# Down projection of a streaming encoder's feed-forward layer: from eight block products to seven, with the weight sums made in device memory

## The chip, the cores and the metric

The kernel runs on one core of a Trainium2 chip. The metric is the device time of one execution in microseconds. Before the change the median of three runs is 1411.47 us (1410.40 to 1413.36).

## The reference, cut to what matters

One inference step of a one-layer encoder: a mixer (three kinds of gated recurrences), then a convolutional feed-forward layer, each between two RMS norms. There are 1024 prompt rows and 32 sample rows, D_MODEL is 1024 and D_FF 2816. All arrays are fp32. The change is in the last step, the product with `w_down`, and what follows it:

```
def conv_ffn(xn, buf, w_up, conv_w, conv_b, w_down):
    up = xn @ w_up
    up, buf = causal_dwconv(up, buf, conv_w, conv_b)
    gate, val = jnp.split(up, 2, axis=-1)
    return (jax.nn.gelu(gate, approximate=True) * val) @ w_down, buf
...
        h, ffn_buf = conv_ffn(rms_norm(x, g_ffn_pre[l]), states[6][l], ffn_w_up[l], ffn_conv_w[l],
                              ffn_conv_b[l], ffn_w_down[l])
        x = x + rms_norm(h, g_ffn_post[l])
```

So the down projection is (1056 x 2816) times (2816 x 1024), then a norm over each row of 1024 and the residual.

## The kernel before

The kernel is written with a planner: the program names tiles in pools, and the planner places them, sets the order of each engine's instructions from dependencies, priorities (the order of writing) and its own timeline, and adds the waits. `tc.issue_after` is the hand-written way to keep an instruction behind another one; it is used in a few places, none of them in the down projection. SP issues nearly all DMAs, in one queue.

Every large product is made in fp32r from split operands. `split` writes a high half with ACT (a cast) and a low half with DVE (source minus high half), and `mm3` multiplies high by high, high by low and low by high into one PSUM bank. A block of 128 x 128 by 128 x N thus costs three products of TensorE.

The stages in order:

- The input projection and the mixer fill the first 690 us. The input projection's weights come from device memory, are split, and the low halves are stored there (`lt_d`, `lf_d`) and read again for the later groups of rows.
- The up projection runs from about 690 to 1146 us. `up_all` goes over 22 blocks `f` of 128 hidden columns (a gate and a value block each) and over two halves `s` of the rows. Each block already uses seven products (`PROD`) instead of eight on quarter blocks; the sums of its weights are made by DVE in SBUF (`up_operands`). `up_finish` does the convolution, the gelu and the product, with four small POOL copies ahead of each ACT step, and stores block `f` of the hidden rows to `h_d[f]` (128 hidden x 1060 columns of rows, the prompt in two halves with a gap, the sample in the middle).
- The down projection `down_all` takes three groups of rows (`DGROUPS`): (0, 1, 8), (2, 3, 4) and (5, 6, 7), where 8 is the sample. For each group it goes over the 22 hidden blocks again: `load_h` loads that group's rows of `h_d[f]` and all of `w_dn[f]` (512 KB), and splits them. In the first group the weights are the stationary operand and 288 rows are streamed, so the result is transposed back afterwards (`turned`); in the other two groups the rows are stationary and 512 weight columns are streamed. `finish` does the norm and the residual (`residual` loads rows of `x2_d`). In the last group the last four blocks are kept back (`n_end`) and applied bank by bank, so that the banks close one after the other.

The tag `raw` holds two raw weight tiles, `op` seven split ones. `ahead` prepares the first two blocks of the down projection while the up projection ends.

Of the kernel before, what the change touches and what calls it, by code (L numbers as in the profile page):

```python
# [18 lines left out]
SEQ = 1024  # L19
DEC = 32  # L20
# [14 lines left out]

DGROUPS = [(0, 1, 8), (2, 3, 4), (5, 6, 7)]

# [53 lines left out]
def body(ctx: ExitStack, tc: tile.TileContext, a: dict):  # L91
# [45 lines left out]
    h_d = dr.tile([NF, 128, NCOL], F32, name="h_d")  # L137

# [1203 lines left out]
    def up_all(pw_, W0, X, uus, py, ahead, begun):  # L1342

        raw, W = {}, {0: W0}
        late = None
        for f in range(NF):
# [3 lines left out]
            for s in range(2):  # L1350
# [25 lines left out]
    def load_h(ph, g, f, spans, w, deep=None):  # L1376
        r = ph.tile([128, 384], F32, tag="hr", name=f"hr{g}_{f}", bufs=2)
        for (c0, c1, o) in spans:
            sp.dma_start(r[:, o:o + c1 - c0], h_d[f, :, c0:c1])
        hh = ph.tile([128, 384], F32R, tag="hh", name=f"hh{g}_{f}", bufs=4)  # L1380
        hl = ph.tile([128, 384], F32R, tag="hl", name=f"hl{g}_{f}", bufs=4)
        split(hh[:, :w], hl[:, :w], r[:, :w], dve)
        wr = praw[0].tile([128, 1024], F32, tag="raw", name=f"wd{g}_{f}r", bufs=2)
        sp.dma_start(wr, a["w_dn"][f])
        return hh, hl, [weight_halves(f"wd{g}_{f}{hf}", wr[:, 512 * hf:512 * hf + 512], deep) for hf in range(2)]

    def spans_of(us):
        spans, off, w = [], {}, 0
        for u in us:
            n = 128 if u < 8 else DEC  # L1390
            off[u] = w
            if spans and spans[-1][1] == fcol(u):
                spans[-1][1] += n
            else:
                spans.append([fcol(u), fcol(u) + n, w])
            w += n
        return spans, off, w

    def down_all(ph, p6, gp, begun):
        xres = {}  # L1400

        def residual(u):
            n = 128 if u < 8 else DEC
            x = p6.tile([128, 1024], F32, tag="xres", name=f"fr{u}", bufs=4)
            sp.dma_start(x[:n], x2_d[128 * u:128 * u + n, :])
            xres[u] = x

        def finish(u, n, src):

            x = xres.pop(u)  # L1410
            ss = p6.tile([128, 4], F32, tag="fss", name=f"gss{u}", bufs=4)
            jk = p6.tile([128, 1024], BF16, tag="fjk", name=f"gjk{u}", bufs=2)
            ys = []
            for hf in range(2):
                c = slice(512 * hf, 512 * hf + 512)
                act.activation(jk[:n, c], src[hf], AF.Square, accum_out=ss[:n, 2 + hf:3 + hf])  # L1416
                y = p6.tile([128, 512], F32, tag="yt", name=f"yt{u}{hf}", bufs=4)
                dve.tensor_tensor(y[:n], src[hf], gp[:n, c], op=ALU.mult)
                ys.append(y)
            pool.tensor_tensor(ss[:n, 0:1], ss[:n, 2:3], ss[:n, 3:4], op=ALU.add)  # L1420
            rstd_of(ss[:n, 1:2], ss[:n, 0:1], n, 1, 1024)
            for hf in range(2):
                c = slice(512 * hf, 512 * hf + 512)
                dve.scalar_tensor_tensor(x[:n, c], ys[hf][:n], ss[:n, 1:2], x[:n, c], op0=ALU.mult, op1=ALU.add)
                sp.dma_start(a["yp"][128 * u:128 * u + n, c] if u < 8 else a["ys"][:, c], x[:n, c])

        def banks_of(g, m):

            where = [(psf, "xw", 4)] * 4 + [(psb, "big", 3)] * 3 + [(psf, "sx", 1)]
            return [p.tile([128, 512], F32, tag=t, name=f"pd{g}_{i}", bufs=b) for i, (p, t, b) in enumerate(where[:m])]  # L1430


        us = DGROUPS[0]
        spans, off, w = spans_of(us)
        banks = banks_of(0, 8)
        for f in range(NF):
            hh, hl, wd = begun.pop(f, None) or load_h(ph, 0, f, spans, w)
            if f == NF - 4:
                for u in us:
                    residual(u)  # L1440
            for d in range(8):
                c = slice(128 * (d % 4), 128 * (d % 4) + 128)
                mm3(banks[d][:, :w], [t[:, c] for t in wd[d // 4]], (hh[:, :w], hl[:, :w]), f == 0, f == NF - 1)
        acc = p6.tile([128, 8, 288], F32, name="accd")
        for d in range(8):
            (act.copy if d % 2 else dve.tensor_copy)(acc[:, d, :], banks[d][:, :w])

        def turned(u):
            n = 128 if u < 8 else DEC
            src = []  # L1450
            for hf in range(2):
                p, t, b = ((psb, "big", 3), (psf, "sx", 1))[hf]
                ps = p.tile([128, 512], F32, tag=t, name=f"pt{u}{hf}", bufs=b)
                for d in range(4):
                    pe.transpose(ps[:n, 128 * d:128 * d + 128], acc[:, 4 * hf + d, off[u]:off[u] + n], ident)
                src.append(ps[:n])
            finish(u, n, src)

        todo = [lambda u=u: turned(u) for u in us]
        for g, us2 in enumerate(DGROUPS[1:], 1):  # L1460
# [10 lines left out]
            for f in range(NF):  # L1471
                ops = load_h(ph, g, f, spans, w, p6 if f >= NF - n_end // 2 else None)
                if f == NF - 4:
                    for u in us2:
                        residual(u)
# [286 lines left out]
```

## Time and profile before

| | |
|---|---|
| median of three runs | 1411.47 us |
| span of the profiled execution (the page gives no other time of it) | 1409.0 us |
| TensorE busy | 1366.7 us, 97% |
| DVE busy | 1009.7 us, 72% |
| ACT busy | 711.2 us, 50% |
| POOL busy | 299.0 us, 21% |
| moved by DMA | 255.10 MB, mean 181 GB/s |
| first and last product of the down projection | 1146.27 us, 1402.27 us |

The page divides the span into 40 slices of 35 us. In its rows a digit is the busy share of a slice in tenths. A group's line ends with the idle time of its engine just before the group's instructions and with what ended most of it. SPq is SP's queue of DMA issues.

### The profile page before, as it was taken

How to read it: one execution, taken by the hardware profiler on the slowest of the kernel's cores; microseconds unless marked ns; L12 is line 12 of the kernel's file. 1: busy time of each engine (PE TensorE's matmuls, PEld its weight loads, DVE VectorE, ACT ScalarE, POOL GpSimd, SP SyncE). 2: the span in 40 equal slices, each digit the busy share in tenths (PEclk: the TensorE clock that was granted, in tenths of full speed). 3: DMA queues.
4: the chain of work that ended last, by engine and by line, in shares of the span. 5: the costliest groups of instructions: out<-in, count | busy, mean ns of one | idle time of the engine just before them, and what ended most of it. 6: DMA issues, size and time to landing. Idle time of an engine off the chain costs nothing.

```text
span 1409.0 us, 30015 instructions
## 1 busy us (share of the span) xinstructions
PE 1366.7 (97%) x11804; PEld 1252.3 (89%) x11804; DVE 1009.7 (72%) x1818; ACT 711.2 (50%) x1399; POOL 299.0 (21%) x497
## 2 busy tenths in 40 slices
PE   6999999999999999999899999999999999999998
PEld 5999889898888987777799999999999999988886
DVE  4786478758687669777798788788878865654644
ACT  4555447445474545334755555455545445543432
POOL 5532311235211245212131111111111110000100
PEclk9999999999999989999999999999999999999999
DMA  9599879785899744445312222222122267764752
GB/s 346 191 335 351 273 236 304 229 273 189 271 274 347 243 160 142 137 135 144 123 55 96 99 82 76 77 79 88 63 91 77 70 208 224 245 220 166 247 177 101
DMA packets 129444, 255.10 MB, mean 181 GB/s; under 512 B 27639, under 2 KB 74263, under 8 KB 129303
## 3 DMA queue, kind: packets, MB, share of 16 engines
q1 hardware_dynamic: 122839, 244.54, 52.2%
q10 hardware_dynamic: 4800, 4.33, 0.9%
q0 software_dynamic: 1664, 4.33, 0.8%
q8 instruction: 92, 1.51, 0.4%
q14 instruction: 49, 0.40, 0.1%
HBM read 192.26 MB, written 60.89 MB: 180 GB/s over the span
## 4 chain that ended last, share of the span: by engine, by line
PE 79%; DVE 9%; DMA 4%; ACT 4%; issue 2%; POOL 1%; SPq 1%; DVEq 0%; POOLq 0%; ACTq 0%
PE pd L102 6%; PE pd L101 6%; PE pd L100 6%; PE pux L100 4%; PE pux L102 4%; PE pux L101 4%; PE pv L100 4%; PE pv L102 4%; PE pv L101 4%; PE puw L101 3%; PE puw L100 3%; PE puw L102 3%; PE mi L718 2%; PE zp L100 2%; PE zp L102 2%; PE zp L101 2%
## 5 line engine op out<-in xcount | busy, mean ns | idle before, releaser
L1336 DVE SCALAR_TENSOR_TENSOR y<-uu,fconv_sb,y 128x1060 f32<-128x1060 f32 x88 | 116.3, 1321 | 28.3 <-ACT y L1334 27.6
L102 PE MATMUL pd<-wd,hl 128*128 128x512 f32 x264 | 105.0, 399 | 0.0
L101 PE MATMUL pd<-wd,hh 128*128 128x512 f32 x264 | 104.1, 394 | 0.0
L100 PE MATMUL pd<-wd,hh 128*128 128x512 f32 x264 | 103.4, 393 | 0.0
L1330 POOL COPY uu<-uu 128x2 f32<-128x2 f32 x44 | 36.7, 834 | 214.4 <-DVE uu L1278 214.2
L1273 ACT COPY c<-pux 128x274 f32<-128x274 f32 (+1 forms) x132 | 49.3, 376 | 40.8 <-PE pux L102 39.8
L100 PE MATMUL pv<-wt_0h,xh 128*128 128x256 f32 (+2 forms) x195 | 57.8, 297 | 6.8 <-ACT xh L319 4.8
L1334 ACT ACTIVATE y<-uu,fconv_sb 128x1060 f32<-128x1060 f32 x44 | 56.1, 1275 | 16.0 <-POOL uu L1331 15.4
L100 PE MATMUL zp<-woh,ch 128*128 128x512 f32 (+1 forms) x144 | 59.2, 412 | 1.9 <-DVE z L1154 1.2
L101 PEld LDWEIGHTS pd<-wd,hh 128*128 128x128 f32 x264 | 49.6, 188 | 12.8
L100 PEld LDWEIGHTS pd<-wd,hh 128*128 128x128 f32 x264 | 49.6, 188 | 11.6
L102 PEld LDWEIGHTS pd<-wd,hl 128*128 128x128 f32 x264 | 49.6, 188 | 11.4
L101 PE MATMUL zp<-wol,ch 128*128 128x512 f32 (+1 forms) x144 | 57.9, 402 | 0.0
L102 PE MATMUL zp<-woh,cl 128*128 128x512 f32 (+1 forms) x144 | 57.8, 403 | 0.0
L102 PE MATMUL pv<-wt_0h,xl 128*128 128x256 f32 (+2 forms) x195 | 56.8, 291 | 0.4 <-DVE xl L320 0.4
L101 PE MATMUL pv<-wt_0l,xh 128*128 128x256 f32 (+2 forms) x195 | 56.4, 289 | 0.1
L102 PE MATMUL pv<-wt_1h,xl 128*128 128x256 f32 (+2 forms) x195 | 56.4, 289 | 0.0
L101 PE MATMUL pv<-wt_1l,xh 128*128 128x256 f32 (+2 forms) x195 | 56.2, 288 | 0.0
L100 PE MATMUL pv<-wt_1h,xh 128*128 128x256 f32 (+2 forms) x195 | 56.1, 288 | 0.0
L1420 POOL TENSOR_TENSOR gss<-gss 128x1 f32<-128x1 f32 (+1 forms) x9 | 2.6, 293 | 243.6 <-ACT gjk L1416 243.6
L100 PE MATMUL pd<-hh,wd 128*128 128x288 f32 x176 | 52.0, 296 | 0.0
L101 PE MATMUL pd<-hl,wd 128*128 128x288 f32 x176 | 52.0, 296 | 0.0
(1682 smaller groups left out, 5204.1 us busy)
## 6 DMA issues: line engine op xcount, KB each, us to landing
h_d<-y SPq DMA_DIRECT2D x22, 530.0 KB, 2.8
wt_0r<-in_w_tok SPq DMA_DIRECT2D x21, 512.0 KB, 5.8
wt_1r<-in_w_tok SPq DMA_DIRECT2D x21, 512.0 KB, 6.7
wt_0l<-lt_d SPq DMA_DIRECT2D x14, 512.0 KB, 4.3
wt_1l<-lt_d SPq DMA_DIRECT2D x14, 512.0 KB, 6.6
hr<-h_d SPq DMA_DIRECT2D x44, 128.0 KB, 3.3
hr<-h_d SPq DMA_DIRECT2D x22, 192.0 KB, 3.6
x<-in_xp SPq DMA_DIRECT2D x8, 512.0 KB, 8.6
```

The costliest lines, as they stand in the source:

```text
L100: pe.matmul(ps, lh[0], rh[0], start=first, stop=False, **kw)
L101: pe.matmul(ps, lh[0], rh[1], start=False, stop=False, **kw)
L102: return pe.matmul(ps, lh[1], rh[0], start=False, stop=last, **kw)
L718: fn(*args, **kw)
L1273: kept[name] = act.copy(t, ps)
L1330: pool.tensor_copy(u[:, GAP_P:GAP_P + 2], u[:, GAP_S - 2:GAP_S])
L1334: act.activation(y, u, AF.Identity, scale=fconv[:, j, 2:3], bias=fconv[:, j, 3:4])
L1336: dve.scalar_tensor_tensor(y, uu[i][:, s:s + NCOL], fconv[:, j, s:s + 1], y, op0=ALU.mult, op1=ALU.add)
L1420: pool.tensor_tensor(ss[:n, 0:1], ss[:n, 2:3], ss[:n, 3:4], op=ALU.add)
```

## The change

The rows of the prompt are halved (512 and 512), the hidden dimension is halved (11 and 11 blocks of 128) and the output columns are halved (512 and 512). The eight products of half by half become seven (`P1` to `P7`), each over 11 hidden blocks, with four PSUM banks of 128 rows x 512 columns. Sums of rows are made by DVE in place on resident row tiles: all 22 blocks of `h_d` stay in SBUF (`ht`). Sums of weights are made before, in device memory: `sum_weights` issues copies from SP and accumulating DMAs from POOL into four arrays `ws_d`, in 48 steps whose calls are spread over the blocks of the up projection. The results collect in `CA` and `CB` in SBUF. The sample's 32 rows are a stationary operand of 64 columns of their own (their high and low halves side by side), multiplied in `P1` and `P2` with the same weight tiles; the two halves are added by four small fp32 products with a selection matrix `sel`. The seven tiles `op` still hold split weights; split rows take four tiles `hop`. `freed` releases the up projection's first column operands while its last block runs and starts loading rows there; `y` tiles move to the other side of SBUF. The last product `P3` closes the upper half of the rows during its first four blocks and the lower half bank by bank over its last four.

```
+    ws_d = dr.tile([4, 128, NF // 2, 512], F32, name="ws_d")
...
+    def up_all(pw_, W0, X, uus, py, freed, ahead, begun):
...
                     blk = up_block(pw_, f, s, W[f], X[s], uu)
                     next(blk)
                     next(late, None)
+                    if f == NF - 1 and s == 1:
+                        freed()
+                    m = (2 * f + s - 3) * len(SUMS) // 34
+                    while len(summed) < min(m, len(SUMS)):
+                        sum_weights(*SUMS[len(summed)])
+                        summed.append(m)
...
+    NP = NF // 2
+    H2 = GAP_P + 2
+
+    def sum_weights(t, n, q):
+
+        def src(k, j):
+            return a["w_dn"][NP * k + q:NP * k + q + n, :, 512 * j:512 * j + 512].rearrange("f p n -> p f n")
+
+        ta, tb, tc_, td = (ws_d[i, :, q:q + n] for i in range(4))
+        (lambda: sp.dma_start(ta, src(0, 0)),
+         lambda: sp.dma_start(tb, src(0, 1)),
+         lambda: pool.dma_start(ta, src(0, 1), accum_op=ALU.add),
+         lambda: pool.dma_start(tb, src(1, 1), accum_op=ALU.add),
+         lambda: sp.dma_start(tc_, ta),
+         lambda: pool.dma_start(tc_, src(1, 1), accum_op=ALU.add),
+         lambda: sp.dma_start(td, tc_),
+         lambda: pool.dma_start(td, src(1, 0), accum_op=ALU.add))[t]()
+
+    SUMS = [(t, min(2, NP - 2 * i), 2 * i) for _, t, i in
+            sorted((2 * i + 3 * t, t, i) for i in range((NP + 1) // 2) for t in range(8))]
...
+    def load_h(pool_, f):
+        hts[f] = pool_.tile([128, NCOL], F32, name=f"ht{f}")
+        sp.dma_start(hts[f], h_d[f])
+
+    def ablk(i, k, p):
+        h = hts[p + NP * k]
+        return h[:, 512 * 0:512] if i == 0 else h[:, H2:H2 + 512]
+
+    ASRC = dict(P1=(0, 0), P2=(0, 1), P4=(1, 1), P6=(0, 0), P5=(1, 1), P7=(1, 0), P3=(0, 1))
...
+    def down_operands(ph, kind, p, early=False):
+        down_raw(kind, p)
+        h = halves_of(ablk(*ASRC[kind], p), f"{kind}h{p}", ph, "hop", 4)
+        wp = (ph, "hop", 4) if early else (praw[1], "op", 7)
+        if kind in ("P1", "P2"):
+            r = wraws[kind, p]
+            w = [halves_of(r[:, j], f"{kind}w{p}{j}", *wp) for j in range(2)]
+        else:
+            w = [halves_of(wraws[kind, p // 2][:, p % 2], f"{kind}w{p}", *wp)]
+        return h, w
+
+    def sample_operands(pc, k):
+        r = pc.tile([128, NP, DEC], F32, tag="hsr", name=f"hsr{k}", bufs=2)
+        sp.dma_start(r, h_d[NP * k:NP * k + NP, :, SMP:SMP + DEC].rearrange("f p n -> p f n"))
+        t = pc.tile([128, NP, 2, DEC], F32R, tag="hso", name=f"hso{k}", bufs=2)
+        act.copy(t[:, :, 0, :], r)
+        dve.tensor_tensor(t[:, :, 1, :], r, t[:, :, 0, :].bitcast(F32), op=ALU.subtract)
+        return t
+
+    def sample_products(ps, t, p, w):
+
+        for part in range(2):
+            for j in range(2):
+                pe.matmul(ps[j][:2 * DEC], t[:, p].rearrange("q e n -> q (e n)"), w[j][part],
+                          start=p == 0 and part == 0, stop=p == NP - 1 and part == 1)
+
+    def down_all(ph, pc, begun, late):
...
+        for f in range(NP):
+            load_h(ssp, f)
...
+        def run(kind, banks, first, last, each=None, n_end=0):
+            end = []
+            for p in range(NP):
+                ops = begun.pop((kind, p), None) or down_operands(ph, kind, p)
+                if p >= NP - n_end:
+                    end.append((p, ops))
+                    continue
+                h, w = ops
+                wi = w[0]
+                for i in range(4):
+                    c = slice(128 * i, 128 * i + 128)
+                    mm3(banks[i], (h[0][:, c], h[1][:, c]), wi, first and p == 0, last and p == NP - 1, skip_group_check=True)
+                if each:
+                    each(p, w)
+            return end
+
+        def combine(p):
+            f0, f1 = hts[p], hts[p + NP]
+            a11, a21, a22 = f0[:, :512], f0[:, H2:H2 + 512], f1[:, H2:H2 + 512]
+            dve.tensor_tensor(a22, a21, a22, op=ALU.subtract)
+            dve.tensor_tensor(a21, a11, a21, op=ALU.subtract)
...
+        s_ops = sample_operands(pc, 1)
+        s1 = [psf.tile([128, 512], F32, tag="xw", name=f"s1{j}", bufs=4) for j in range(2)]
+        W = w_banks("q2")
+        run("P2", W, True, True, lambda p, w: sample_products(s1, s_ops, p, w))
...
+        run("P1", X, True, False, lambda p, w: sample_products(s2, s_ops0, p, w))
...
+            pe.matmul(o[:DEC], sel, keep1[:, j], start=True, stop=False)
+            pe.matmul(o[:DEC], sel, keep2[:, j], start=False, stop=True)
...
+        run("P4", W, True, True, lambda p, w: combine(p))
...
+        run("P6", X, False, False, lambda p, w: p + 1 < NP and second_sum(p + 1))
...
+        run("P5", W, True, True, lambda p, w: fourth_sum(p))
...
+        run("P7", X, False, True)
+        late.close()
...
+        def each(p, w):
+            if p < 4:
+                upper_half(p)
+                norm_of(p, 128, CA[:, p, 0], 0, ss_of[p])
+
+        end = run("P3", W, True, True, each, 4)
+        for i in range(4):
+            c = slice(128 * i, 128 * i + 128)
+            for p, (h, w) in end:
+                mm3(W[i], (h[0][:, c], h[1][:, c]), w[0], False, p == NP - 1, skip_group_check=True)
+            dve.tensor_tensor(CA[:, i, 1], CA[:, i, 1], W[i], op=ALU.add)
+            norm_of(i, 128, CA[:, i, 1], 1, ss_of[i])
+            close(i, 128, [CA[:, i, hf] for hf in range(2)], xres[i], ss_of[i])
...
+    def freed():
+        pxs.close()
+        ph.append(phs.enter_context(tc.tile_pool(name="ph", bufs=1, side="left")))
+        for f in range(NP, NF - 1):
+            load_h(ph[0], f)
 
     def ahead():
-        spans, _, w = spans_of(DGROUPS[0])
-        for f in range(2):
-            begun[f] = load_h(py[0], 0, f, spans, w)
+        for p in range(1):
+            begun["P2", p] = down_operands(ph[0], "P2", p, True)
...
+    load_h(ph[0], NF - 1)
     sp.dma_start(a["p_fc"], fhalo)
     sp.dma_start(a["q_fc"], fcache)
```

The steps of `SUMS` are ordered by 2 i + 3 t, where `t` is the step of one sum's chain and `i` the pair of hidden blocks; a step writes 512 KB, or 256 KB for the last single block. The prediction also names lines that the change leaves alone: the input projection's loads and stores (151, 250, 329, 341), the start-up load of line 173, the mixer's load of its operands (730) and its cleared first state (760), and, among those it replaces, the residual loads (1405), the down projection's weight loads (1384) and the back transposes (1455).

More of the change, by code (lines that the diff above doesn't have):

```diff
@@ L1387, in spans_of @@
[L1387 to L1419, printed above, removed]
@@ L1433, in down_all @@
[L1433 to L1443, printed above, removed]
@@ new lines, in down_all @@
+        for i in range(4):
+            dve.tensor_tensor(CA[:, i, 0], CA[:, i, 0], X[i], op=ALU.add)
+        W = w_banks("q4")
+        run("P4", W, True, True, lambda p, w: combine(p))
+        for i in range(4):
+            act.copy(CB[:, i, 0], W[i])
+        for j in range(2):
+            norm_of(8, DEC, y8[j], j, ss8)
+        close(8, DEC, y8, xs8, ss8)
+        second_sum(0)
+        run("P6", X, False, False, lambda p, w: p + 1 < NP and second_sum(p + 1))
+        for i in range(4):
+            act.copy(CA[:, i, 1], X[i])
```

162 lines of the change are left out of this document (96 added, 66 removed).

## Prediction

> **What bounds the kernel now.** I read the page first, then the busy time by stage, then the chain of waits in the stages that the change touches. The page:
>
> ```profile
> span 1409.0 us, 30015 instructions
> ...
> PE 1366.7 (97%) x11804; PEld 1252.3 (89%) x11804; DVE 1009.7 (72%) x1818; ACT 711.2 (50%) x1399; POOL 299.0 (21%) x497
> ...
> PE   6999999999999999999899999999999999999998
> ...
> DMA  9599879785899744445312222222122267764752
> ...
> PE 79%; DVE 9%; DMA 4%; ACT 4%; issue 2%; POOL 1%; SPq 1%; DVEq 0%; POOLq 0%; ACTq 0%
> ```
>
> TensorE is busy in nearly every slice. The DMA engines are full in the first third, nearly empty in the up projection (slices 21 to 32) and half full in the down projection. By stage (PE, PEld, DVE, ACT, POOL busy; granted clock; DMA share; GB/s), with the down projection in the last two rows:
>
> ```profile
> 10.00:80.00 70.00, 63.73 (x370) 58.81 (x371) 47.45 (x58) 34.85 (x59) 35.99 (x18) 1.00 0.78 274
> 80.00:200.00 120.00, 116.23 (x1112) 110.30 (x1111) 76.59 (x140) 64.26 (x129) 31.75 (x46) 1.00 0.89 307
> 200.00:300.00 100.00, 99.27 (x1105) 91.57 (x1104) 80.35 (x188) 58.51 (x113) 21.46 (x31) 1.00 0.82 262
> 300.00:500.00 200.00, 194.31 (x2519) 175.91 (x2518) 143.11 (x370) 108.10 (x248) 55.05 (x84) 0.97 0.78 260
> ...
> 1146.27:1215.07 68.80, 68.80 (x519) 68.80 (x517) 42.24 (x72) 34.78 (x69) 2.13 (x4) 1.00 0.78 248
> 1215.07:1402.69 187.62, 187.59 (x818) 150.85 (x816) 96.23 (x161) 76.75 (x161) 8.74 (x24) 1.00 0.57 191
> ```
>
> The down projection is 256.4 us of TensorE without a gap. At the other end of the kernel the picture differs. The chain of waits in the first 140 us, by line:
>
> ```profile
> by line: PE pv L100 7.1%; PE pv L102 7.1%; PE pv L101 6.7%; issue 6.7%; DMA x<-in_xp 6.2%; DMA wf_5r<-in_w_feat 5.3%; DMA qkb<-qkb_d 5.1%; DMA wf_8r<-in_w_feat 5.0%; DVE e L517 4.4%; DMA mqk_d<-y 3.8%; DMA wf_2r<-in_w_feat 3.7%; DVE y L390
> ```
>
> The transfers named add to 29.1%, 41 us of 140: there the chain runs through the DMA queue.
>
> **TensorE's work in the down projection.** The price of one product is its distance from the next: with 288 moving columns, with 512 (two pieces of the chain of waits), and of eight transposes:
>
> ```profile
> 1180.00 0.30 PE L101 MATMUL pd<-hl,wd 128*128 128x288 f32 x1
> ...
> 1181.33 0.30 PE L102 MATMUL pd<-hh,wd 128*128 128x288 f32 x1
> ```
>
> ```profile
> 1271.54 0.24 PE pd L102
> 1272.24 0.24 PE pd L102
> ```
>
> ```profile
> 1220.67 1.03 PE L1455 MATMUL pt<-ident,accd 128*128 128x128 f32 x8
> ```
>
> 288 columns: ten products in 1.33 us, 0.133 each. 512 columns: the chain's two rows are the same one of three products, 0.70 us apart, so 0.2333 each. Before: 22 blocks x 24 = 528 of the first kind (70.4 us), 2 x 22 x 18 = 792 of the second (184.8), 24 transposes (8 in 1.03): 258, where the trace has 256.4. After: seven products x 11 blocks x 12 = 924, and 2 x 11 x 4 = 88 for the sample rows, all with 512 columns: 1012 x 0.2333 = 236.1. The sample rows alone cost 20.5 of it; before they were 32 of 288 columns, 7.8 us. Four more products add up the sample's high and low rows in plain fp32; priced by the transposes (0.13 per 128 columns) they take 0.52 each, and four passes of 0.2333 would be 0.93: 2.1 to 3.7 us, I take 2.7. TensorE's sum is 238.8, a gain of **17.6 us** if it never waits.
>
> **DVE and ACT beside it.** Per split of 512 columns:
>
> ```profile
> L109 DVE TENSOR_TENSOR wd<-wd_3r,wd 128x512 fp32r<-128x512 f32 x6 | 4.1, 687 | 2.5 <-ACT wd L106 2.5
> L106 ACT CAST wd<-wd_2r 128x512 fp32r<-128x512 f32 x6 | 3.7, 620 | 1.0 <-DMA wd_2r<-in_w_dn 0.6 <-PE puw L102 0.3
> ```
>
> P1 and P2 need three splits a block, 2.06 us of DVE against 16 x 0.2333 = 3.73 of TensorE. P4 needs two splits and two row sums, 4 x 0.69 = 2.75 against 12 x 0.2333 = 2.80: covered, with nothing to spare, and the sample's closing and the CA sums (about 5 us of DVE) fall into it; P6 and P5 (three, 2.06 of 2.80) pay that back through the four operands held ahead. P3 has only two splits a block, but the closing of four row tiles (some 13 us) and eight sums out of PSUM (5.5) in its first blocks, 11.2 us long. That pile is 20 us of DVE work beside P3's operands; the slack of P7 and P3 (1.4 us a block) takes most: I charge **3 us** (0 to 7). Handing PSUM banks over behind ACT's copies at P2 to P1 and P1 to P4: **2 us** (0 to 4). The end of the kernel gets one more sum ahead of its square: **1 us**, since today's chain after the last product is square, two POOL steps, DVE, store.
>
> **The head of the down projection.** Today the first down product starts with no gap, its rows stored long before. The new P2 wants its sample rows of all of h_d[11:22], so it needs the last store (KB each and median us to landing, then the issue of that store):
>
> ```profile
> h_d<-y SPq DMA_DIRECT2D x22, 530.0 KB, 2.8
> ...
> lt_d<-wt_0l SPq DMA_DIRECT2D x7, 512.0 KB, 5.3
> ...
> hr<-h_d SPq DMA_DIRECT2D x22, 64.0 KB, 3.4
> ```
>
> ```profile
> 1156.31 0.49 SPq L1340 DMA_DIRECT2D h_d<-y  x1
> ```
>
> 1156.3 + 2.8 + 3.4 and two short operations end near 1163.5. Seven weight tiles and two borrowed ones let P2 run five blocks without the sample, 5 x 2.80 = 14 us from 1146.3, to 1160.3. So it waits at least 3 us. Behind the row loads it waits longer: 22 x 530 KB and P2's weights, 11.7 + 5.8 MB, are wanted within 50 us, 350 GB/s, where no stage above moved more than 307. Eleven row loads queued ahead of the sample rows would make it 3 + 17 = 20 us. I take **7 us** (3 to 20), near the row that shows no queue, because only a few row tiles wait for the same late space.
>
> Down projection: -17.6 + 3 + 2 + 1 + 7 = **-4.6 us**.
>
> **The weight sums.** The change issues 48 transfers, 24 copies from SP and 24 accumulations from POOL, 8 x 2.88 = 23.1 MB, written between the up projection's blocks. There they would be free: the DMA row of the page shows 0.2, and POOL mostly waits:
>
> ```profile
> L1330 POOL COPY uu<-uu 128x2 f32<-128x2 f32 x44 | 36.7, 834 | 214.4 <-DVE uu L1278 214.2
> ```
>
> But the place in the program is not the place on the chip. These rows show what the planner does with an instruction that needs nothing:
>
> ```profile
> 3.80 0.27 DVE L760 MEMSET S<- 128x256 f32 x1
> ```
>
> ```profile
> 102.98 0.32 SPq L730 DMA_DIRECT2D qkb<-qkb_d  x1
> ```
>
> ```profile
> 1146.84 0.90 SPq L1405 DMA_DIRECT2D fr<-x_d  x2
> ...
> 1154.16 0.34 SPq L1384 DMA_DIRECT2D wd_5r<-in_w_dn  x1
> ```
>
> SP's issues at the end of the start-up loads, and one of its waits (us, times, longest):
>
> ```profile
> 12.88 0.43 SPq L250 DMA_DIRECT2D gh<-in_grows  x1
> 13.44 0.35 SPq L151 DMA_DIRECT2D x<-in_xp  x1
> ```
>
> ```profile
> SPq L173 <- DMA gx<-in_grows: 0.9, 1, 0.9
> ```
>
> The memset stands in the mixer behind the load of line 730 and ran 99 us ahead of it. The residual rows of line 1405 are asked for at the nineteenth block of the first pass and were issued before the sixth block's weights, as soon as their space was free. The sums need no space: the first twelve copies read an input and write device memory, so nothing holds them after the last start-up load, at 12.88. I expect them in SP's order between the last two issues quoted, ahead of the first feature weights, and each later step as soon as its predecessor lands. Queued behind them on SP: x, the `lt_d` and `lf_d` stores, the `wf` weights, for all of which TensorE waits (chain above). SP also stops at its ninth transfer until the first has landed (L173 waited for gx, eight issues earlier), so it cannot run past slow copies. On POOL, the halves of the `wf` weights and the `rs` steps queue behind each accumulation's wait.
>
> Their price: the stage at 80 to 200 us moved 307 GB/s at share 0.89, 345 at full share, so 23.1 MB cost 67 us of full DMA if an accumulation costs as a copy. If it costs two, since it must fetch the old sum too, 100; with a third, 134. The free share up to 300 us is 0.22 x 70 + 0.11 x 120 + 0.18 x 100 = 46.6 us; up to 500, 44 more. So the delay is 67 - 46.6 = 20 us, 54 or 87, and with the slack up to 500 as little as 5, as the first twelve copies (5.8 MB, 17 us) stand in front of everything whatever follows. No row prices an accumulation; I take the middle of 20 and 54, **37 us** (5 to 87).
>
> The Trainium skill's "DMA: Bandwidth & Descriptors" (Anatomy of one DMA) gives 2.0 us plus bytes/436e3; at that rate the sums would take 53 us and the delay would be 6, but no stage here reached it. The same page (Rules for kernel authors) says that an accumulate reads its destination and writes it later, which speaks for the 54.
>
> Sum: -4.6 + 37 = +32.4. The profiled execution spans 1409.0; the page lists no further time around it, and the median of the runs is 2.5 us more. On the median: 1411.5 + 32.4 = **1444 us** (own range 1412 to 1494).
>
> **The rivals.** (1) *The sums stay in the up projection and are hidden.* For it: some 34 half blocks with DMA share 0.2; the program's order would have to hold, against the rows of lines 760 and 1405. Then only the down projection counts: 1411.5 - 4.6 = **1407 us**, faster; 1398 to 1426 by the bounds of the waits. It decides if the copies stand behind 700 us in SP's order. (2) *Hidden sums, but the sample rows queue behind all the row loads at P2's head*, 20 us instead of 7: 1407 + 13 = **1420 us**. For it: the loads are written ahead of the sample's; against it: they need space of different ages. (3) *Sums in the up projection whose waits stop POOL*: POOL's four copies per block go ahead of ACT's `y`, and a wait in front of them holds `uu`. One exposed landing (the 5.3 us of `lt_d`, the same size) in four or five blocks gives about **1430 us**; against it, the steps of one sum are written some three half blocks apart.
>
> **How the numbers follow.** Forecast 0.62, rival 1 0.25, rival 2 0.08, rival 3 0.05. A measurement of this kernel tells 0.2%, 2.8 us, from no change. Rival 1 gives faster 0.14, within 0.07, slower 0.04; all but 0.01 of the rest is slower: faster 0.15, same 0.07, slower 0.78. The range goes from 1401 (leaving out a quarter of rival 1) to 1486 (a tenth of the forecast's case, where accumulations cost three copies).
>
> **What would show it.** Right: `ws_d` transfers from about 13 us on; TensorE's first slices emptier and every later stage shifted by some 37 us; the up projection as dense as now; the down projection 1012 products at 0.2333 within about 252 us, with a gap near its head until the sample rows land. Wrong: `ws_d` first seen after 700 us, or seen early with TensorE's first 140 us unchanged; a down projection above 270 us would mean that P2's head or DVE in P4 and P3 was undersized.

## The result, and the profile after

The kernel after takes **1506.47 us** (median of four runs, 1500.16 to 1506.96) against 1410.93 us for the kernel before in the same comparison: a ratio of 1.067 (95% interval 1.065 to 1.069). That is slower, as forecast, but by 95.5 us where 32.4 were forecast, and above the range's end of 1486. The profiled execution took 1506.92 us and spans 1505.1, against 1409.0 before: 96.1 us to explain.

The page of the kernel after, in the rows that were shown of before:

```profile
span 1505.1 us, 29146 instructions
PE 1374.9 (91%) x11480; PEld 1234.2 (82%) x11480; DVE 1039.2 (69%) x1859; ACT 725.6 (48%) x1398; POOL 322.9 (21%) x521
PE   3775799999999999999979999999999985999996
DMA  9999988697678974443522222222222277433353
```

TensorE's first five slices have fallen from 6 9 9 9 9 to 3 7 7 5 7, and there is a new hole at slices 33 and 34 (8 and 5). The up projection between them (slices 22 to 32) is as dense as it was. Where each stage begins and ends, from the groups of TensorE's products (line, operation, count, shortest, median and longest ns, first and last start), in the kernel after:

```profile
L97 PE MATMUL pux<-B11h,A_0h x8: 287/339/415, 756.9 to 779.7; 128*128 128x274 f32 x4, 128*128 128x256 f32 x4
L97 PE MATMUL q<-P2w,P2h x44: 390/394/796, 1223.0 to 1290.8; 128*128 128x512 f32 x44
L97 PE MATMUL x<-P1w,P1h x44: 393/394/398, 1292.5 to 1331.7; 128*128 128x512 f32 x44
L99 PE MATMUL q<-P3w,P3h x44: 390/393/502, 1461.0 to 1491.5; 128*128 128x512 f32 x44
```

and the first of them in the kernel before, which for the down projection began at 1146.27:

```profile
L100 PE MATMUL pux<-B11h,A_0h x8: 282/291/415, 680.5 to 702.7; 128*128 128x274 f32 x4, 128*128 128x256 f32 x4
```

The first of these groups is taken as the mark of the up projection's start; one other group of its first block starts some 13 us ahead of it in both kernels (667.2 and 743.5). So the up projection starts **76.4 us** later (756.9 against 680.5) and itself takes 466.1 us against 465.8. The down projection takes 268.8 us (1223.0 to 1491.5 and one product) against 256.4, **12.4** more. The tail behind the last product is 13.3 against 6.3, **7.0** more. 76.4 + 0.3 + 12.4 + 7.0 = 96.1.

**The start.** SP's issues, in order of time:

```profile
12.78 0.43 SPq L248 DMA_DIRECT2D gh<-in_grows  x1
13.25 1.34 SPq L1389 DMA_DIRECT2D ws_d<-in_w_dn  x2
14.73 0.52 SPq L149 DMA_DIRECT2D x<-in_xp  x1
15.29 0.60 SPq L1390 DMA_DIRECT2D ws_d<-in_w_dn  x1
```

The first copy goes out at 13.25, between the two issues that the prediction named. The last accumulation is issued at 158.8; such a transfer lands some 12 us after its issue (the median), so the sums are over by some 170 us. The busy time by stage (columns as in the prediction):

```profile
20.00:60.00 40.00, 17.63 (x99) 15.55 (x100) 3.72 (x5) 9.13 (x17) 9.24 (x9) 0.70 1.06 315
60.00:100.00 40.00, 29.41 (x133) 26.55 (x132) 18.27 (x28) 14.68 (x24) 25.14 (x17) 0.80 1.08 281
100.00:140.00 40.00, 28.38 (x132) 26.13 (x131) 16.62 (x25) 11.48 (x19) 18.13 (x16) 0.88 1.06 303
```

For 120 us the DMA share is above 1.0, DVE and ACT wait, and TensorE runs 17 to 29 of 40 us, at a granted clock of 0.70 to 0.88 on top.

**The head of the down projection.** The issues of SP around P2's start, and the busy time there:

```profile
1236.54 0.33 SPq L1338 DMA_DIRECT2D h_d<-y  x1
...
1239.85 10.51 SPq L1423 DMA_DIRECT2D ht<-h_d  x12
1251.35 0.37 SPq L1449 DMA_DIRECT2D hsr<-h_d  x1
1252.74 4.86 SPq L1411 DMA_DIRECT2D wrP<-in_w_dn  x1
```

```profile
1240.00:1250.00 10.00, 6.94 (x27) 4.92 (x25) 2.68 (x4) 2.90 (x5) 0.00 (x0) 0.95 1.01 351
1250.00:1260.00 10.00, 0.00 (x0) 0.00 (x0) 0.00 (x0) 0.00 (x0) 0.00 (x0) 0.57 1.04 401
1260.00:1270.00 10.00, 6.84 (x20) 3.83 (x21) 4.33 (x7) 3.86 (x7) 0.00 (x0) 0.58 0.47 113
```

Twelve row loads go out between the last store and the sample read. From 1250 to 1260 nothing computes and the DMA engines are full. TensorE's own waits in P2 (who waits, for what: us, times, longest; "issue" means that the view names no releaser, and here the sample's halves `hso` were made just before it ended):

```profile
PE s L1459 <- issue: 14.6, 1, 14.6
PE q L97 <- ACT P2w L103: 5.4, 2, 3.8
```

P2 takes 69.5 us up to P1's first product (1223.0 to 1292.5), where its 176 products need 41.1 at 0.2333 each. The wait for the sample is 14.6 of the difference, the waits for weight tiles 5.4. The other six products together, P1 to P3, take 199.2 us (1292.5 to 1491.7) for 836 x 0.2333 + 2.7 = 197.7 us of work.

### The profile page after: what moved, and what is told of

The parts are those of the page before. It is cut to its first block, busy times and chain, and to the rows that moved or that the text cites. A ratio compares the mean times of both kernels' runs of the same rounds, so it can differ in the third digit from the quotient of the medians.

```text
span 1505.1 us, 29146 instructions
## 1 busy us (share of the span) xinstructions
PE 1374.9 (91%) x11480; PEld 1234.2 (82%) x11480; DVE 1039.2 (69%) x1859; ACT 725.6 (48%) x1398; POOL 322.9 (21%) x521
## 3 DMA queue, kind: packets, MB, share of 16 engines
HBM read 207.08 MB, written 83.95 MB: 193 GB/s over the span
## 5 line engine op out<-in xcount | busy, mean ns | idle before, releaser
L1328 POOL COPY uu<-uu 128x2 f32<-128x2 f32 x44 | 28.8, 654 | 213.1 <-DVE uu L1276 212.9
L1271 ACT COPY c<-pux 128x274 f32<-128x274 f32 (+1 forms) x132 | 49.5, 376 | 40.4 <-PE pux L99 39.4
L97 PEld LDWEIGHTS pv<-wt_0h,xh 128*128 128x128 f32 (+1 forms) x195 | 38.4, 198 | 33.7 <-ACT xh L317 22.7
L1331 POOL COPY fhalo<-uu 128x2 f32<-128x2 f32 x44 | 16.5, 376 | 169.9 <-DVE uu L1276 169.9
L427 POOL TENSOR_TENSOR vg<-vth,gh 128x256 f32<-128x256 f32 (+1 forms) x36 | 31.0, 862 | 85.0 <-DVE vth L423 60.7
L811 DVE COPY_PREDICATED P<-masks_sb,sc 128x352 f32<-128x352 int32 (+1 forms) x44 | 29.8, 678 | 20.4 <-PE sc L716 20.1
L388 DVE SCALAR_TENSOR_TENSOR y<-pc,mconv_sb,y 128x384 f32<-128x384 f32 (+1 forms) x45 | 28.8, 643 | 19.7 <-ACT y L386 18.3
L216 POOL TENSOR_SCALAR hrs<-hss 128x5 f32<-128x5 f32 (+3 forms) x27 | 8.8, 326 | 152.5 <-DVE hss L918 151.0
L99 PEld LDWEIGHTS pv<-wt_0h,xl 128*128 128x128 f32 (+1 forms) x195 | 38.6, 198 | 1.4 <-DVE xl L318 1.0
L98 PEld LDWEIGHTS pv<-wt_0l,xh 128*128 128x128 f32 (+1 forms) x195 | 38.6, 198 | 1.2 <-DVE wt_0l L106 0.5
```

The lines of the kernel that those rows point to most:

```text
L97: pe.matmul(ps, lh[0], rh[0], start=first, stop=False, **kw)
L98: pe.matmul(ps, lh[0], rh[1], start=False, stop=False, **kw)
L99: return pe.matmul(ps, lh[1], rh[0], start=False, stop=last, **kw)
L388: dve.scalar_tensor_tensor(y, pc[:, s:s + L], mconv[:, j, s:s + 1], y, op0=ALU.mult, op1=ALU.add)
L427: pool.tensor_tensor(o[:n], th[:n], gh[:n, c0:c0 + 256], op=ALU.mult)
L811: dve.copy_predicated(dst, mk.broadcast_to([n, 11, *mk.shape[2:]]), src)
```

## The experiments

All edits are to the kernel after; the cuts of code are shortened. "First up product" is the mark used above, read from each profile. The kernels were run in five sets, each beside the kernel before, whose median differs from set to set (1409.39 to 1411.60 us). So a difference of some 2 us between kernels of different sets is not read from their medians, but from the lengths of stages in the profiles.

### Where the sums run

Each transfer is held behind the up projection's own instructions; `spq` is the latest up-weight load on SP, `plq` the latest halo copy on POOL.

```diff
-  sum_weights(*SUMS[len(summed)])
+  with tc.issue_after(kept["spq"].ins), tc.issue_after(kept["plq"].ins):
+      sum_weights(*SUMS[len(summed)])
```

> The kernel after, with each weight-sum transfer held on its queue behind the up projection's own instructions of the half block in which it is written (a weight load on SP, a halo copy on POOL). Theory (the 76.5 us ahead of the up projection come from where the sums run, and there is room for them later): the first up product is back at 680 us, the up projection keeps its 20.6 us per block, total 1506.5 - 76.5 = 1430 us (1425 to 1436). Rival (the sums cost what they cost wherever they run, by POOL's waits in front of the halo copies or by DMA): the up projection grows by 10 us or more, total above 1440.

Measured: 1426.69 us (1424.42 to 1428.21), a ratio of 1.011 to before (1.009 to 1.013), as the theory had it. The paced kernel's rows:

```profile
L97 PE MATMUL pux<-B11h,A_0h x8: 287/353/580, 678.9 to 701.7; 128*128 128x274 f32 x4, 128*128 128x256 f32 x4
L97 PE MATMUL q<-P2w,P2h x44: 392/394/796, 1141.7 to 1208.3; 128*128 128x512 f32 x44
```

The up projection starts at 678.9 and takes 462.8 us (678.9 to 1141.7), no more than before, while the sums run beside it. The whole delay of the start was the place of the sums. What is left, 15.5 us over the kernel before (1411.22 in this set), is the down projection and the tail.

Two kernels let part of the sums float to the start again; `t` counts the eight steps of a sum, of which 0 and 1 are the first copies, 2 and 3 the first accumulations.

```diff
+  if SUMS[len(summed)][0] > 1:    # the second of the two kernels: > 3
       (hold behind spq and plq as above)
```

> As the paced kernel, but the first twelve copies (5.8 MB, needing nothing) are left free to float to the start; accumulations and later copies are held. Theory (bytes ahead of the critical start-up loads): 5.8 MB at 345 GB/s in front of everything, 17 us over the paced kernel. Rival (what costs is the accumulations and the waits that they put on POOL's and SP's queues): under 8 us over the paced kernel.

> As before it, but the first twelve accumulations float too, 24 of 48 steps. The profile after shows 24 accumulations at 4.3% of the span of sixteen engines, 64 us for 11.5 MB, so an accumulation costs about twice a copy. Theory (the full price of the transfers, twice for an accumulation, part of it in the slack): 32 us more DMA than with the twelve copies, between 20 and 35 us more in the total. Rival (accumulations cost as copies): 10 to 17 us more.

A third one is the kernel after with `accum_op=ALU.add` taken from the four lines of POOL's transfers: it leaves the additions out, so it does not compute the layer, and its bytes and their order stay.

> The kernel after with the 24 accumulations replaced by plain copies on the same queue at the same places, so the weights are not summed; bytes written and order as after. Theory (an accumulation costs two copies): the sums' load falls by some 32 us and the total to about 1475 (1465 to 1485). Rival (what costs is the order in SP's and POOL's queues and the landing of each step): the total stays above 1495.

Measured: 1438.9, 1459.57 and 1478.41 us, one run each. The first up product, in us (among the kernels with paced sums it varies between 678.3 and 681.7):

| sums ahead of the start | first up product | delay against paced | load on the DMA engines |
|---|---|---|---|
| none (paced) | 678.9 | 0 | 0 |
| 12 copies | 691.2 | 12.3 | 15.7 |
| 12 copies, 12 accumulations | 709.7 | 30.8 | 48.5 |
| 48 copies | 728.1 | 49.2 | 62.9 |
| 24 copies, 24 accumulations (after) | 756.9 | 78.0 | 97.0 |

The load comes from the queue that POOL's transfers use (packets, MB, share of sixteen engines), in before, in after and with plain copies:

```profile
q0 software_dynamic: 1664, 4.33, 0.8%
```

```profile
q0 software_dynamic: 7680, 15.86, 5.1%
```

```profile
q0 software_dynamic: 4864, 15.86, 2.9%
```

Before, the queue took 0.008 x 1409.0 = 11.3 us of all engines. After it takes 76.8, so 24 accumulations take 65.5, **2.73 us** each; as plain copies, with the same bytes, 0.029 x 1476.6 - 11.3 = 31.5, **1.31** each. An accumulation costs 2.1 copies. (The load of SP's copies in the table is an estimate at the same 1.31.) In the paced kernel the queue's share is 5.7% of 1422.6, 69.8 us without before's 11.3, 2.91 each, so an accumulation costs no less where the DMA share is 0.36 to 0.60 (the paced kernel from 700 to 1100 us): the price is its own, not that of the crowd.

With twelve copies ahead the theory gave 17 us and 12.2 came, less than the theory and more than its rival's 8. With twelve accumulations too it held (20.7 us more in the total, at the low end of 20 to 35), and with plain copies it held (1478 against 1475). The rival there, that queue order alone makes the delay, is out: the same steps in the same order cost 28 us less without the addition.

The last test of the place releases all 48 transfers at the start of the up projection, without pace:

```diff
-  with tc.issue_after(kept["spq"].ins), tc.issue_after(kept["plq"].ins):
+  with tc.issue_after(kept["spq0"].ins), tc.issue_after(kept["plq0"].ins):   # first up weights, first memset
```

> The kernel after with all 48 weight-sum transfers released at the start of the up projection and not paced, held only behind that stage's first weight load on SP and its first memset on POOL. Theory (delay is the sums' transfers less the slack of the stage in which they run, with SP's and POOL's queues in order): 100 us of transfers run as one block with about half of the DMA free, and the next weight loads and the halo copies stand behind them; up projection 20 to 50 us longer, total 1450 to 1477. Rival (the place alone decides, pace does not matter): as the paced kernel, 1424 to 1430.

Measured: 1459.06 us in one run, within the theory's 1450 to 1477. The busy time by stage and the waits of this kernel (who waits, for what: us, times, longest):

```profile
710.00:730.00 20.00, 17.18 (x115) 16.96 (x116) 14.21 (x19) 7.64 (x13) 7.38 (x10) 0.84 1.10 248
730.00:750.00 20.00, 14.86 (x100) 14.45 (x98) 8.12 (x11) 4.95 (x7) 3.72 (x7) 0.84 1.11 233
750.00:770.00 20.00, 13.61 (x92) 12.98 (x92) 9.45 (x14) 6.86 (x11) 6.98 (x12) 0.76 1.08 302
```

```profile
POOL ws_d L1397 <- DMA ws_d<-ws_d: 20.3, 5, 9.0
ACT y L1332 <- POOL uu L1329: 17.9, 5, 6.8
ACT A_2h L103 <- DMA wu2r<-in_w_up: 12.2, 1, 12.2
```

Even in the stage where the page shows a DMA share of 0.2, the sums in one block cost 32 us (the up projection takes 494.6 us, 680.3 to 1174.9, instead of 462.8): the DMA engines are full for 60 us, POOL stands at an accumulation's wait in front of the copies for `uu`, and the up weights queue behind. Place and pace both count.

### The head of the down projection

First the sample read alone is put ahead of the eleven late rows:

```diff
+  s_ops = sample_operands(pc, 1)
+  with tc.issue_after(kept["hsr"].ins):      # the sample's DMA
       for f in range(NP):
           load_h(ssp, f)
```

> The paced kernel, with the read of P2's sample rows issued on SP ahead of the eleven late row loads (held behind it) instead of behind them. Theory (the gap at P2's head is the sample read queued behind the rows): the last store's landing at 1158.5, a read of 3.5 us and two short operations bring the first sample product to about 1165, while five blocks keep TensorE busy until 1156; the gap is 9 to 10 us instead of about 26, total 1426.7 - 16 = 1410.5 us (1406 to 1415). Rival (the late space or the transfers around it hold P2, not the order): less than 6 us gained, or the gap comes again at P1's head, where the rows are wanted.

Measured: 1424.98 us (1423.14 to 1426.86), a ratio of 1.011, the same as paced. P2 up to P1's first product falls from 68.2 to 66.3 us in the profiles. The theory is wrong as it stands: the gain is the rival's, under 6 us. SP's issues, and the waits from 1148 to 1192:

```profile
1159.12 0.37 SPq L1450 DMA_DIRECT2D hsr<-h_d  x1
1159.55 10.34 SPq L1424 DMA_DIRECT2D ht<-h_d  x11
1170.93 0.33 SPq L1412 DMA_DIRECT2D wrP<-in_w_dn  x1
```

```profile
ACT P2w L103 <- DMA wrP<-in_w_dn: 17.9, 6, 12.2
PE q L97 <- ACT P2w L103: 16.7, 3, 10.6
```

The sample read is out in time, and the gap has only changed its cause: P2 now stops at its sixth block, whose weight tile stands behind the same rows. Reading the sample in two parts (ten h tiles early, the eleventh behind the last store) runs into the same wall.

```diff
+  begun["s1"] = sample_rows(ph[0], 0, NP - 1)                       # before the last up block is finished
...
+  sample_rows(ph[0], NP - 1, NP, *begun["s1"])                      # behind the last store
```

> The paced kernel, with P2's sample rows read in two parts: ten of the eleven h tiles before the last up block is finished, the eleventh behind the last store and ahead of the late row loads; tiles in space that is free early. Theory (P2 waits only because one read covers also the last h tile): P2 has no gap, total 1426.7 - 26 = 1401 us (1398 to 1405), before the tail is mended. Rival (weights and late rows, 17 MB wanted in 50 us, bind next): a gap of 8 us or more stays at the head of P2 or P1, total above 1409.

Measured: 1424.10 us (1421.90 to 1426.71): the rival's result. P2 stops for 12.1 us at that weight tile and takes 65.6 us:

```profile
PE q L97 <- ACT P2w L103: 12.1, 1, 12.1
PE s L1470 <- DVE hso L1463: 5.6, 1, 5.6
```

The new theory: 5.8 MB of rows that P1 wants 30 us later stand ahead of everything that P2 needs. Two late rows are then held behind each of P2's weight loads from the sixth on:

```diff
+  if kind == "P2" and p > 4:
+      with tc.issue_after(kept["wr"].ins):       # this block's weight load
+          for f in range(2 * p - 10, min(2 * p - 8, NP)):
+              load_h(ssp, f)
```

> The paced kernel, with the eleven late row loads held two by two behind P2's weight loads from the sixth on (and so behind the sample read as well). The sample read ahead of the rows alone gave under 2 us, since the sixth weight tile then stood behind the same rows. Theory (what holds P2 is 5.8 MB of rows for P1, wanted 30 us later, ahead of everything that P2 itself needs): only the sample's own lateness is left, 9 to 10 us; P2 falls from 66.6 us to about 51, total 1426.7 - 15.5 = 1411 us (1407 to 1415). Rival (P2's weights are slow for another reason, two buffers and the transfers' rate): above 1420, or a gap moves to P1.

> Rows behind P2's weights and the sample rows in two reads. Theory: the two causes at P2's head are one behind the other, each alone hidden by the other; with both gone P2 takes 41 us and what short waits remain (6 us of DVE's sample halves), total 1426.7 - 20 = 1407 us (1402 to 1411). Rival (the rows are then late for P1): P1 has gaps, above 1412.

Measured: 1413.31 us (1411.27 to 1416.36) and 1410.59 us (1407.56 to 1413.16; ratio 1.0004, 0.9990 to 1.0017). Both lie in their ranges, 2 and 4 us above the values given. P2 takes 56.5 and 53.6 us, where it took 68.2 and 65.6 with the rows in front, so most of the gap was the rows. The split read takes 2.6 us off P2 with the rows in front and 2.9 behind them.

So P2 was still longer than the 47 us that the second theory gave. The next kernel also stages the ten early rows (two, then the first sample read, then P2's third and fourth weights with the rest behind them). With it goes a second edit, the scaling of the closing norm's weights on ACT held behind the sample's last cast; no run separates the two.

```diff
+  if kind == "P2" and p in (2, 3):
+      down_raw(kind, p)
+      with tc.issue_after(kept["wr"].ins):
+          for f in range(NP + 2, NP + 5) if p == 2 else range(NP + 5, NF - 1):
+              load_h(ph, f)
```

> The kernel with split sample read and staged late rows; now also the ten early rows are staged: two of them, then the first sample read, then P2's third and fourth weight tiles with the other rows behind them; the scaling of the closing norm's weights is held behind the sample's last cast on ScalarE. Theory (a third read behind rows: the sample read of 1144.4 landed 10.3 us later behind ten row loads, and TensorE waited 6 us for it, and the third weight tile came as late): P2 takes 41 to 44 us instead of 50, total 1410.6 - 7 = 1403.5 us (1400 to 1407). Rival (the last h tile's lateness is what is left): P2 stays at 48 us or more, total above 1408.

Measured: 1406.99 us (1404.59 to 1411.39; ratio 0.9981, 0.9966 to 0.9997). The total fell by half of what the theory said. P2 stays long, as the rival had it, but not for the rival's reason: the waits for the sample are gone, yet P2 takes 52.8 us. TensorE waits for weights for 6.7 us up to 1190, with the DMA engines full, and its products are slower behind the waits (busy time in one stretch, with a granted clock of 0.74, and the waits):

```profile
1170.00:1180.00 10.00, 5.97 (x19) 4.16 (x18) 1.99 (x3) 2.35 (x5) 0.00 (x0) 0.74 1.02 416
```

```profile
PE q L97 <- ACT P2w L103: 6.7, 3, 4.0
```

The next theory: what is left is bytes, all 22 rows and 11 weight tiles in P2's time. The last kernel puts one row behind each weight load, from P2's eighth to P1's seventh, instead of two behind each of P2's from the sixth on (it has the tail's edit, below, as well):

```diff
+  rows = {("P2", 7): (0,), ("P2", 8): (1,), ("P2", 9): (2,), ("P2", 10): (3,)}.get((kind, p), ())
+  if kind == "P1" and p + 4 < NP:
+      rows = (p + 4,)
```

> As the kernel before it (rows last, P3's end bank by bank), with the eleven late rows one behind each weight load, four in P2 and seven in P1, instead of all within P2. Theory (what is left at P2 is DMA bandwidth: 17.7 MB of rows and weights in the 46 us before P2's end, at a share of 1.0): P2 falls from 49.3 us to 42 to 44, P1 keeps its 41 to 42, total 1406.3 - 6 = 1400 us (1397 to 1404). Rival (the order of single weights, or P1 then waits for its rows): P2 and P1 together stay within 2 us, total above 1404.

Measured: **1399.39 us** (1398.52 to 1403.40), against 1411.60 for the kernel before: a ratio of 0.992 (0.990 to 0.994). The theory held: P2's first group runs from 1143.4 to 1185.5, 42.1 us, where the theory gave 42 to 44. The rows of this kernel:

```profile
L97 PE MATMUL q<-P2w,P2h x44: 388/392/503, 1143.4 to 1185.5; 128*128 128x512 f32 x44
L97 PE MATMUL x<-P1w,P1h x44: 388/394/501, 1188.4 to 1229.5; 128*128 128x512 f32 x44
L99 PE MATMUL q<-P3w,P3h x44: 388/394/502, 1355.3 to 1387.8; 128*128 128x512 f32 x44
```

Up to P1's first product P2 takes 45.0 us, P1's group takes 41.1 where it took 41.3 in the kernel with the early rows staged, and the whole down projection 244.6 us (1143.4 to 1388.0) against 256.4 before.

### The tail

In the kernel after, the last four blocks of P3 are written bank by bank, but the planner mixed the banks, so all four end nearly together. VectorE at its end (start, us, line, operation; in brackets its idle time and what ended it):

```profile
1490.34 1.88 DVE L1607 TENSOR_TENSOR ca<-ca,q 128x512 f32<-128x512 f32 x3 [5.26 <-PE q L99]
...
1499.78 2.08 DVE L1523 SCALAR_TENSOR_TENSOR fr<-ca,gss,fr 128x512 f32<-128x512 f32 x3 [0.72 <-POOL gss L217]
```

DVE idles 5.26 us and then has all four row tiles to close. The edit keeps the order as written, on the paced kernel:

```diff
+  with tc.issue_after(prev.ins) if i else ExitStack():
       for p, (h, w) in end:
-          mm3(W[i], ...)
+          prev = mm3(W[i], ...)
```

> The paced kernel, with the last four blocks of P3 held on TensorE in the order in which they are written, bank by bank. Theory (the 7 us after the last product come from four banks that end together and queue their closing on DVE and POOL): only the last row tile closes after the last product, 13.4 us fall to about 7, total 1426.7 - 6.5 = 1420 us (1418 to 1423). Rival (the closing chain of one row tile is that long by itself): within 2 us of the paced kernel.

> Paced sums, sample rows in two parts, and P3's end bank by bank. Theory (three independent causes, gains add): 1401 - 6.5 = 1394.5 us (1391 to 1399), faster than the kernel before by 1.2%. Rival (with the head closed, DVE's pile in P4 or P3 becomes the bound and takes part of it back): above 1402.

> As before it, and P3's end bank by bank, which alone gave 1.4 us from the first down product to the end. Theory: 1405 us (1400 to 1410), faster than the kernel before by 0.3%. Rival (the head's gap and the tail were hiding DVE's pile): no gain over the kernel with the two head edits alone.

> As before it, with P3's end bank by bank. Theory: 1.5 us less, 1402 us (1399 to 1406), faster than the kernel before by 0.5%. Rival (P3's DVE pile takes back what the tail gives): no difference to the kernel without this edit.

Measured: 1424.63 us (1422.34 to 1425.52; ratio 1.011, the same as paced), where 1420 was expected, with the split sample 1422.31 (1419.95 to 1424.36), where 1394.5 was expected, with the staged rows 1411.91 (1405.92 to 1414.54), where 1405 was expected, and with the early rows staged too 1406.28 (1402.33 to 1411.71; ratio 0.998, 0.996 to 0.999), where 1402 was expected. None of the four lies in its theory's range. In the first of them the tail falls from 13.4 to 9.9 us, but P3's products now take 33.3 us from first to last where they took 31.2. The bank that goes first needs the operands of all four last blocks at once, and DVE, busy with the closing of the upper rows, makes the last of them at 1404.16, 24 us after P3's start:

```profile
1404.16 0.69 DVE L106 TENSOR_TENSOR P3h<-ht,P3h 128x512 fp32r<-128x512 f32 x1
1405.44 0.69 DVE L1609 TENSOR_TENSOR ca<-ca,q 128x512 f32<-128x512 f32 x1 [0.59 <-PE q L99]
...
1418.86 1.41 DVE L1524 SCALAR_TENSOR_TENSOR fr<-ca,gss,fr 128x512 f32<-128x512 f32 x2 [0.99 <-POOL gss L217]
```

So the net gain between the two profiles is 1.4 us, and even then the tail is 3.6 us longer than the 6.3 of the kernel before; what makes up that rest was not tested. In the other three pairs of kernels with and without this edit the median is 1.8 and 0.7 us lower and 1.3 higher, within the spread of their runs. That the shorter tail is paid for by the longer P3 is read from the profile; no run separates them.

## Why the prediction was right or wrong, point by point

| step of the prediction | forecast | measured |
|---|---|---|
| weight sums float to the start, behind 12.88 | yes | yes, 13.25 |
| delay by them | +37 (5 to 87) | +76.4 |
| TensorE's work in the down projection, with the bank handover | -17.6, +2 | -15.0 with all short waits |
| DVE's pile in P3 | +3 (0 to 7) | 0 (2 when the banks keep their order) |
| head of P2 | +7 (3 to 20) | +27.4 |
| tail | +1 | +7.0 |
| up projection | 0 | +0.3 |

(P2 up to its last product takes 68.5 us, 27.4 more than its 41.1; the -15.0 is the rest of 268.8 - 256.4.) The forecast was 32.4 us and 96.1 came in the profiles. Of the 63.7 us between them the delay by the sums is 39.4, the head of P2 20.4 and the tail 6.0; the other terms give 2.1 back.

**The mechanism was right, its size was not.** That the sums would leave their place in the program was the forecast's main claim, and the paced kernel shows that it is the whole of the start's delay. The mis-sized step is "the delay is 67 - 46.6 = 20 us, 54 or 87" and the middle of 20 and 54. First, the load: with an accumulation at 2.1 copies it is 97 us, the prediction's 100, so its branch of 54 was the right one; it had taken a value below for want of a row. The Trainium skill's "DMA: Bandwidth & Descriptors" (Rules for kernel authors) had said that an accumulate reads its destination and writes it later. The queue's 2.1 times the time for the same bytes fits that, but no row shows the second read: the page counts 207.08 MB read from device memory with the additions and without them. Second, the slack: the prediction gave the sums all that the DMA engines had free up to 300 us. The transfers stand ahead of the stage's own in both queues and were over by some 170 us. By then the kernel had done what before had done by 95, and in before the free share to that point is 0.12 x 20 + 0.17 x 40 + 0.20 x 35 = 16 us, by before's rows:

```profile
0.00:20.00 20.00, 10.52 (x54) 9.39 (x55) 13.68 (x27) 9.58 (x17) 12.83 (x25) 1.00 0.88 294
20.00:60.00 40.00, 38.46 (x232) 35.36 (x231) 21.13 (x22) 19.44 (x32) 18.11 (x9) 1.00 0.83 302
60.00:100.00 40.00, 36.30 (x228) 35.00 (x227) 35.81 (x49) 22.62 (x38) 18.71 (x13) 1.00 0.80 270
```

97 - 16 = 81, near the 76.4. The 95 was found with the measured delay, so this shows that the sizes agree and is no forecast. Slack counts only where the transfers lie beside it. How much of the 76.4 is bytes, how much the order in SP's and POOL's queues and how much the lower granted clock (0.70 to 0.88) stays open, since all three lie in the same stretch; the burst kernel shows full engines and waits in both queues at work together.

**The head.** The second failed step is the 7 us taken "near the row that shows no queue, because only a few row tiles wait for the same late space". Twelve row loads went out ahead of the sample, and the rival that put the sample behind them (chance 0.08, as a case without the start's delay) was right in its mechanism, beside the forecast's own. The wait for the sample alone was 14.6 us, nearer to its 20 than to 7. The rest of the 27.4 was in neither price: 5.4 are waits for weight tiles, 1.0 a wait for the up projection's last sums, and most of the 6.4 left are products that came at 0.37 to 0.43 us each, instead of 0.23, behind the gaps. Moving the sample ahead did not help, since the sixth weight tile stood behind the same rows. The prediction had the figure that counted, 17.5 MB wanted within 50 us where no stage moved more than 307 GB/s, and used it only for the queue ahead of the sample.

**Smaller terms.** The tail was taken from the code's order, which the planner did not keep; the same doubt that the prediction had raised for the sums holds there. Keeping the order takes 3.5 us off the tail and puts 2.1 on P3. P3's pile of DVE work was real, but hidden while the banks were mixed. P4 with "nothing to spare" held: TensorE has no gap from 1270 to 1460. The down projection of 268.8 us stayed under the 270 that the prediction had named as the sign of an undersized head, and the head was undersized all the same, so that sign was set too far out.

**What the change is worth.** The price of the seven products was right: P1 to P3 take 199.2 us for 197.7 of work. With sums paced, rows staged, the sample split and P3's end in order, the kernel is 12.2 us faster than before, where the rival without the floating sums gave 4 to 5.

## What to carry to other kernels

An instruction that needs nothing is placed by the planner, not by its line: hold a background transfer behind the first instructions of the stage that is to hide it, on each queue that issues it, and pace it, since 97 us of transfers in one block cost 32 us even where four fifths of the DMA time had been free. Price it at the rate of its own kind (an accumulation into device memory was 2.1 copies here), and set against it only the slack that lies beside it. Where a gap has a queue of loads in front of it, move the loads that are wanted last, not the one that is waited for: moving the read ahead shortened P2 by 1.9 us, moving the rows back behind P2's weights by 11.7.

## What was not expected of the hardware

In these traces a gap of TensorE costs more than its length. In the kernel with the split sample, TensorE stood 12.1 us, and its products then came at almost half the pace for 5 us (pieces of the chain of waits: start, us):

```profile
1186.36 0.43 PE q L99
...
1188.22 0.23 PE q L98
```

Each product takes 0.43 us or more, instead of 0.23, from 1183.0 to 1187.6, so some 2 us are lost behind this gap. The kernel with the sample read first shows the same 0.43 behind its gap of 10.6 us, up to 1188.6. The Trainium skill's "TensorE: Matmul & The Clock Gate" (Why this matters for your kernels) says that idle gaps above some 3 us bring the gate back to half rate; the granted clock of 0.57 and 0.58 (means over 10 us) around the gap of the kernel after agrees. The prediction had charged gaps at their bare length.
